# A two-layer hybrid diffusion step on one core: the order of instructions from another scheduling simulation

## The chip, the cores and the metric

The kernel runs on one core of a Trainium2 chip. The metric is the device time of one execution in microseconds; before the change it is 2791.19 us, the median of 3 runs (2787.31 to 2797.09). Five engines with a queue of instructions each work side by side: TensorE (PE; its weight loads are PEld), VectorE (DVE), ScalarE (ACT), GpSimd (POOL) and SyncE (SP), which here only issues DMAs. Each queue is executed in order, and engines wait for each other through semaphores.

## The reference, cut to what matters

128 context tokens and 128 latent tokens go through two trunk layers with one set of weights. All data is float32.

```python
def trunk_layer(x, cvec, p, l, rope, ctx):
    mods = (silu(cvec) @ p['ada_w'][l] + p['ada_b'][l])         # 6 vectors of 2048
    h = rmsnorm(x, p['norm1_g'][l]) * (1 + scale1) + shift1
    u = h @ p['w_in'][l]                                        # 2048 x 4960
    o_mla, ckv, kr = mla(u_mla, ...)                            # 8 heads, low-rank q and kv, softmax
    o_gdn, s_gdn = gated_deltanet(u_gdn, ...)                   # 4 heads, two directions, chunked delta rule
    o_ssd, s_ssd = mamba2_ssd(u_ssd, ...)                       # 8 heads, two directions, chunked scan
    mixed = concatenate([o_mla, o_gdn, o_ssd], -1) @ p['w_out'][l]
    x = x + gate1 * mixed
    h = rmsnorm(x, p['norm2_g'][l]) * (1 + scale2) + shift2
    gt, up = split(h @ p['ffn_w_gu'][l], 2, -1)                 # 2048 x 11264
    x = x + gate2 * ((silu(gt) * up) @ p['ffn_w_down'][l])      # 5632 x 2048
```

## The kernel before, in words

The activations lie transposed, features on the partitions and the 256 tokens along the free dimension, so a weight block is the stationary operand of a matmul and the tokens stream through.

*Weights.* A weight comes in units of at most 128x1024 floats. `unit` (L372) loads one from DRAM (`load`, L331, on SP's queue, tile `raw`, four buffers), and `split` (L357) makes two parts of it: ScalarE rounds it to the high part `w1` (L360), and VectorE or GpSimd subtracts that from the original to get the low part `w2` (L364); which of the two engines does it is fixed in the program by a share per stage. Each has three buffers. The activations have the same two parts, and a product takes three matmuls or, in the FFN's wide form, two (512 and 256 columns). All matmuls are issued by `mm` (L224, seen as L225). They accumulate in four PSUM banks `acc`; the small matmuls of the recurrences and of attention use three banks `mx`.

*Stages.* Layer 0's input projection lies between 0 and some 240 us, the rest of layer 0's mixing (state space scan, delta rule, attention, output projection) up to about 720 us, its FFN up to about 1490 us, layer 1's projection and mixing up to about 2060 us, and its FFN from there to the end. In the mixing stages chunks of weight matmuls stand beside the chains of the three head groups, some of which go through DRAM (the decay rows `gcd`, the blocks `sB`, `sZ`, `sW` of the triangular solve, the outputs `og`).

*Modulation vectors.* The product of the condition with `ada_w` is spread over the whole program. Some blocks go through TensorE (`ada_run`, L398, tiles `araw`, bank `ada`); the others are multiplied and summed on VectorE during the FFNs (`vec_sums`, L451, the instruction at L505, tile `junk`), paced by `tick` (L531) with constants per stage. Their loads are on SP's queue too, among those of the weights.

*What sets the order.* The program is written in Python in one order. The Tile framework then puts the instructions of each engine into the order in which they are queued. It goes forward in simulated time: when an engine is free in the simulation, it takes, of the instructions whose inputs are there in the simulation, the one of the best priority, and it hands out tile buffers as they come free. The priority is the place in the program; loads and splits of a unit, and the loads of `ada_w`, are put ahead of it (`tc.high_priority()`, L374, L392, L467). Some instructions are tied behind the one traced before them on their engine (`tc.keep_in_program_order`): the first loads (L336), the matmuls while `pinned["on"]` is set (L232: from the first norm until the end of layer 0's projection, and inside a run of `ada` matmuls), and the sums on VectorE (L504).

```python
    def unit(src, nk, n):
        with tc.high_priority():
            raw = raw_tile()
            load(out=raw[:, :nk * n], in_=src)
            w1, w2 = split(raw, nk * n)
```

The context that does this is opened at the end of `kernel` (L1575) without any option, so the simulation is the framework's default one (its core simulator).

## Time and profile before

| | us |
|---|---|
| median of 3 runs | 2791.19 |
| profiled execution | 2789.01 |
| its span, first to last instruction | 2787.2 |
| PE busy | 2624.7 (94%) |
| DVE busy | 1924.1 (69%) |
| ACT busy | 1261.9 (45%) |
| POOL busy | 753.6 (27%) |
| mean granted TensorE clock | 0.981 of full |

A busy share is a mean over all stages, and TensorE's matmuls are pipelined, so a stretch of 50 us with PE busy 100% can still hold fewer matmuls than another. The share of the whole span tells little here; the rows below go by stretch.

### The profile page before, as it was taken

To read this page: it belongs to the slowest core of one execution; us is meant where nothing else is said; L and a number is where in the kernel's file an instruction comes from. 1 tells how busy PE (TensorE), PEld (TensorE's weight loads), DVE (VectorE), ACT (ScalarE), POOL (GpSimd) and SP (SyncE) were. 2 spreads that over 40 slices of the span, in tenths; PEclk is the share of its full clock that TensorE was granted. 3 is DMA by queue.
4 is the path that set the end of the run, shared out by engine and by line. 5 is a ranking of instruction groups with operands and counts; after the bars stand their busy time and mean duration, and the time that the engine had idled before them with its cause. 6 is when DMAs were issued, how large, how long until landed. Compare 5 with 4: busy or idle time off the path is not lost. (4 is left out here: it accounts for less than half of the span.)

```text
span 2787.2 us, 45955 instructions
## 1 busy us (share of the span) xinstructions
PE 2624.7 (94%) x17856; PEld 2324.3 (83%) x17856; DVE 1924.1 (69%) x3162; ACT 1261.9 (45%) x1802; POOL 753.6 (27%) x415
## 2 busy tenths in 40 slices
PE   7988889999999999999999999999999999999999
PEld 5876767888887788788888888888988888888888
DVE  2657845454999899898986786555477777755444
ACT  4345605544444444444334563355454454444333
POOL 1121003222455555455554320231330000000000
PEclk9999999999999999999999999999999999999999
DMA  8988757456698888889985555343657777655554
GB/s 331 347 305 289 251 185 243 151 212 222 230 323 313 312 299 318 294 307 337 340 322 186 172 163 169 111 137 110 221 194 230 232 241 229 202 187 188 195 195 149
DMA packets 224107, 658.01 MB, mean 236 GB/s; under 512 B 34320, under 2 KB 61584, under 8 KB 223888
## 3 DMA queue, kind: packets, MB, share of 16 engines
q1 hardware_dynamic: 174384, 619.26, 64.1%
q10 hardware_dynamic: 49504, 35.81, 4.3%
q8 instruction: 140, 2.29, 0.3%
q14 instruction: 79, 0.65, 0.1%
HBM read 641.22 MB, written 13.76 MB: 235 GB/s over the span
## 5 line engine op out<-in xcount | busy, mean ns | idle before, releaser
L225 PE MATMUL acc<-h,w 128*128 128x256 f32 (+1 forms) x8960 | 1428.9, 320 | 54.2 <-DVE w L364 19.0
L225 PEld LDWEIGHTS acc<-h,w 128*128 128x128 f32 x8960 | 1273.2, 193 | 205.6 <-DVE w L364 29.0
L360 ACT ACTIVATE w<-raw 128x1024 fp32r<-128x1024 f32 (+2 forms) x811 | 828.6, 1025 | 889.1 <-PE acc L225 606.5
L364 DVE TENSOR_TENSOR w<-raw,w 128x1024 fp32r<-128x1024 f32 (+2 forms) x577 | 710.5, 1232 | 512.5 <-ACT w L360 503.6
L364 POOL TENSOR_TENSOR w<-raw,w 128x1024 fp32r<-128x1024 f32 (+3 forms) x234 | 569.2, 2434 | 993.1 <-ACT w L360 840.2
L505 DVE SCALAR_TENSOR_TENSOR junk<-araw,srep 128x1024 bf16<-128x1024 f32 x448 | 544.5, 1215 | 9.6 <-DMA araw<-ada_w 1.9
L225 PE MATMUL acc<-f,w 128*128 128x256 f32 (+1 forms) x2560 | 456.3, 340 | 3.6 <-DVE w L364 3.6
L225 PEld LDWEIGHTS acc<-f,w 128*128 128x128 f32 x2560 | 392.8, 189 | 64.3 <-DVE w L364 4.3
L225 PE MATMUL acc<-m,w 128*128 128x256 f32 x1536 | 191.8, 285 | 0.0
L225 PEld LDWEIGHTS acc<-m,w 128*128 128x128 f32 x1536 | 186.6, 192 | 2.9 <-issue 2.5
L1424 POOL TENSOR_TENSOR f<-sg,f 128x512 fp32r<-128x512 f32 x40 | 60.9, 1523 | 426.3 <-ACT f L1423 426.3
L225 PE MATMUL ada<-araw,sc 128*32 128x256 f32 x1280 | 88.3, 397 | 21.1 <-DVE mods L436 16.2
L225 PE MATMUL mx<-h,w 128*128 128x256 f32 (+1 forms) x672 | 90.7, 293 | 10.1 <-ACT w L360 5.2
L225 PEld LDWEIGHTS mx<-h,w 128*128 128x128 f32 (+1 forms) x672 | 85.7, 195 | 14.6 <-ACT w L360 6.2
L661 DVE SCALAR_TENSOR_TENSOR xT<-acc,mods,xT 128x128 f32<-128x128 f32 x192 | 53.9, 343 | 43.1 <-PE acc L225 35.5
L225 PEld LDWEIGHTS ada<-araw,sc 128*32 128x32 f32 x1280 | 37.6, 112 | 51.8 <-DVE mods L436 18.1
L1428 ACT ACTIVATE up<-acc 128x256 f32<-128x256 f32 x80 | 30.7, 384 | 107.6 <-PE acc L225 76.4
L648 ACT ACTIVATE h<-nt,mods 128x128 fp32r<-128x128 f32 x128 | 44.0, 392 | 63.7 <-DVE nt L647 62.5
L647 DVE SCALAR_TENSOR_TENSOR nt<-xT,modA,rstd 128x128 f32<-128x128 f32 x128 | 57.0, 482 | 7.4 <-ACT rstd L611 7.2
L1428 ACT ACTIVATE sg<-acc 128x256 f32<-128x256 f32 x80 | 29.9, 381 | 68.4 <-PE acc L225 68.4
L602 POOL TENSOR_TENSOR sqacc<-sqacc,sqt 128x256 f32<-128x256 f32 x39 | 39.9, 1022 | 74.0 <-ACT sqt L598 73.1
L1463 DVE TENSOR_TENSOR sg<-sg,up 128x256 f32<-128x256 f32 x80 | 57.8, 723 | 1.6
(296 smaller groups left out, 1971.6 us busy)
## 6 DMA issues: line engine op xcount, KB each, us to landing
araw<-ada_w SPq DMA_DIRECT2D x384, 512.0 KB, 5.4
raw<-ffn_w_gu SPq DMA_DIRECT2D x352, 512.0 KB, 4.4
raw<-ffn_w_down SPq DMA_DIRECT2D x165, 512.0 KB, 4.3
raw<-w_in SPq DMA_DIRECT2D x144, 512.0 KB, 4.6
raw<-w_out SPq DMA_DIRECT2D x64, 512.0 KB, 4.0
raw<-mla_w_uq SPq DMA_DIRECT2D x24, 384.0 KB, 3.1
raw<-mla_w_ukv SPq DMA_DIRECT2D x16, 512.0 KB, 3.7
araw<-srow SPq DMA_DIRECT2D x12, 512.0 KB, 5.7
```

What stands on the lines that cost most here:

```text
L225: return pin(PE.matmul(out, lhsT=lhsT, rhs=rhs, start=start, stop=stop, skip_group_check=True))
L360: S.activation(w1[:, :w], raw[:, :w], AF.Copy)
L364: e.tensor_tensor(w2[:, :w], raw[:, :w], f32(w1[:, :w]), op=ALU.subtract)
L505: V.scalar_tensor_tensor(junk, raw, 1.0, s[r], op0=ALU.mult, op1=ALU.mult, accum_out=sums[g][:, 2 * (c - g[1]) + t, r, h:h + 1]))
L602: G.tensor_tensor(sq["acc"], sq["acc"], t, op=ALU.add)
L647: V.scalar_tensor_tensor(t[:, c], X_["t"][:, kt, c], A[:, kt, g:g + 1], rstd[:, c], op0=ALU.mult, op1=ALU.mult)
L648: S.activation(h1[:, kt, c], t[:, c], AF.Identity, bias=B[:, kt, g:g + 1])
L661: V.scalar_tensor_tensor(xs, ps[:, i * T:(i + 1) * T], gates[:, kt, g:g + 1], xs, op0=ALU.mult, op1=ALU.add)
L1424: G.tensor_tensor(f[:, :, 1], sg_, f32(f[:, :, 0]), op=ALU.subtract)
L1428: S.activation(t, bank[:, NT:2 * NT], AF.Copy)
L1463: V.tensor_tensor(t[:, j], t[:, j], u, op=ALU.mult)
```

## The change

The context in which the kernel is traced is told to schedule with the framework's other simulation, the timeline simulation. Nothing else is changed: the traced program, its priorities, pins, pools and pace constants are the same.

```diff
-    with tile.TileContext(nc) as tc:
+    with tile.TileContext(nc, schedule_with_timeline_sim=True) as tc:
         build(tc, nc, aps)
```

## Rows read from the trace of the kernel before

**Rows 1.** Busy time by stretch; (x) are instructions, PEclk the granted clock.

```profile
core 0: us, PE busy (x) PEld busy (x) DVE busy (x) ACT busy (x) POOL busy (x), PEclk, DMA share, GB/s
0.00:50.00 50.00, 33.20 (x241) 23.63 (x242) 9.69 (x22) 19.43 (x36) 3.67 (x7) 0.90 0.82 317
50.00:350.00 300.00, 268.92 (x2497) 232.44 (x2495) 208.08 (x449) 149.17 (x221) 44.96 (x23) 0.96 0.83 303
350.00:400.00 50.00, 39.47 (x349) 32.26 (x350) 20.92 (x38) 1.36 (x4) 0.00 (x0) 0.90 0.74 228
400.00:750.00 350.00, 322.88 (x2549) 293.53 (x2548) 198.29 (x365) 161.77 (x287) 94.13 (x74) 0.97 0.59 199
750.00:1250.00 500.00, 473.72 (x2639) 403.81 (x2638) 462.57 (x692) 229.64 (x295) 275.04 (x121) 0.99 0.86 310
1250.00:1450.00 200.00, 198.70 (x1125) 172.07 (x1124) 177.60 (x296) 77.38 (x82) 112.45 (x54) 1.00 0.92 333
1450.00:1500.00 50.00, 46.20 (x252) 39.26 (x251) 28.09 (x58) 21.29 (x30) 26.17 (x14) 0.94 0.75 258
1500.00:2067.00 567.00, 525.82 (x4129) 505.11 (x4128) 376.89 (x680) 282.77 (x462) 154.12 (x101) 0.98 0.49 155
2067.00:2787.20 720.20, 715.77 (x4089) 622.17 (x4088) 441.92 (x568) 319.07 (x389) 43.05 (x24) 1.00 0.63 206
```

**Rows 2.** The chain that ended last, its longest pieces: start, us, what.

```profile
1953.39 72.04 PE acc L225 x598
2067.84 715.44 PE acc L225 x4086
```

**Rows 3.** Waits of PE from 50 to 350 us: us in total, times, longest.

```profile
PE ada L225 <- DVE mods L436: 15.6, 7, 4.7
```

**Rows 4.** Waits of PE from 750 to 1250 us.

```profile
PE acc L225 <- DVE w L364: 15.7, 13, 2.8
PE acc L225 <- POOL w L364: 10.4, 13, 1.6
```

**Rows 5.** Groups on DVE, 750 to 1250 us: busy us, mean ns | idle before.

```profile
L505 DVE SCALAR_TENSOR_TENSOR junk<-araw,srep 128x1024 bf16<-128x1024 f32 x252 | 306.4, 1216 | 6.8 <-DMA araw<-ada_w 1.9
L364 DVE TENSOR_TENSOR w<-raw,w 128x1024 fp32r<-128x1024 f32 x65 | 96.7, 1488 | 5.2 <-ACT w L360 4.9
L1463 DVE TENSOR_TENSOR sg<-sg,up 128x256 f32<-128x256 f32 x40 | 40.3, 1006 | 0.8
```

**Rows 6.** Single lines over the whole kernel: duration ns min/median/max.

```profile
L364 DVE TENSOR_TENSOR w<-raw,w x577: 539/1224/3346, 28.0 to 2779.6; 128x1024 fp32r<-128x1024 f32 x171, 128x512 fp32r<-128x512 f32 x13, 128x768 fp32r<-128x768 f32 x7, 128x384 fp32r<-128x384 f32 x2
L364 POOL TENSOR_TENSOR w<-raw,w x234: 1012/2405/3390, 42.2 to 2071.8; 128x1024 fp32r<-128x1024 f32 x111, 128x768 fp32r<-128x768 f32 x3, 128x384 fp32r<-128x384 f32 x2, 128x512 fp32r<-128x512 f32 x1
...
L1463 DVE TENSOR_TENSOR sg<-sg,up x80: 411/425/2674, 777.6 to 2537.2; 128x256 f32<-128x256 f32 x80
```

**Rows 7.** Order of time, 1034 to 1040 us: start, us, instruction [idle before].

```profile
1036.19 2.40 POOL L364 TENSOR_TENSOR w<-raw,w 128x1024 fp32r<-128x1024 f32 x1 [0.60 <-ACT w L360]
...
1036.35 3.33 DVE L364 TENSOR_TENSOR w<-raw,w 128x1024 fp32r<-128x1024 f32 x1
1039.60 1.21 DVE L505 SCALAR_TENSOR_TENSOR junk<-araw,srep 128x1024 bf16<-128x1024 f32 x1
1039.73 0.51 PE L225 MATMUL acc<-h,w 128*128 128x256 f32 x2 [0.80 <-DVE w L364]
```

**Rows 8.** Order of time of PE, 1500 to 2067 us: small groups between chunks.

```profile
1504.31 1.46 PE L225 MATMUL mx<-h,w 128*96 128x256 f32 x11
...
1569.03 0.65 PE L225 MATMUL mx<-da,cst 128*128 128x48 f32 x4 [0.62 <-DVE da L842]
...
1717.96 1.26 PE L225 MATMUL mx<-Z,Bp 128*128 128x128 f32 x8 [4.27 <-DMA Z<-sZ]
...
1949.25 0.41 PE L1346 MATMUL mx<-ident,r 128*128 128x128 f32 x2 [0.23 <-DVE r L1342]
...
2025.37 0.59 PE L225 MATMUL mx<-sqacc,ones 128*128 128x256 f32 x2
```

## Prediction

> **What bounds the kernel now.** I read four views in this order: busy time by stretch, who ended TensorE's waits, the groups of VectorE in the worst-fed stretch, and TensorE's order of time in one mixing stage.
>
> The stretches come first [rows 1]. TensorE is busy nearly all the time from 1250 to 1450 us and from 2067 us to the end, so nothing an order can do there gives much: the last 720.20 us hold 715.77 us of TensorE work. Its gaps lie elsewhere. They are the stretch length less PE busy: 16.8 us in the first 50, 31.1 in 50 to 350, 10.5 in 350 to 400, 27.1 in 400 to 750, 26.3 in 750 to 1250 and 41.2 in 1500 to 2067. With the 9.5 us in the three remaining stretches that is the 162.5 us in which TensorE does nothing. Beside the gaps stands the granted clock: 0.97 in 400 to 750 and 0.98 in 1500 to 2067. A mean of 0.97 says that six hundredths of the stretch ran at the lower of the two levels (1.2 instead of 2.4 GHz), and half of those are lost: 0.03 x 350 = 10.5 us, and 0.02 x 567 = 11.3 us.
>
> What TensorE does at full pace is in the chain of waits [rows 2]: 598 matmuls of w_out in 72.04 us, 120 ns each. The 4129 matmuls of 1500 to 2067 would need 497 us at that pace and take 567. The 70 us between are the 41.2 us of gaps and some 29 us in which TensorE is counted busy but runs slower, the 11.3 us of clock among them.
>
> So the kernel is bound by TensorE's own work, about 2.6 ms, and the order of instructions can only touch what hangs around it.
>
> **The change, part by part.** The flag adds and removes no arithmetic, no transfer and no matmul. The same simulated-time scheduler issues the same instructions; another simulation tells it when an input is ready and an engine free, and with that when a buffer is handed on. As the library describes the two, the new one prices the DMA engines, and the port that VectorE and GpSimd share, as things that are queued for; the old one prices each instruction by itself. What moves is the place of an instruction in its engine's queue, SP's and ScalarE's DMAs included. It matters only where the head of a queue waits while something behind it could run.
>
> *What can't move.* Until layer 0's input projection is done, matmuls are pinned to the order of the program; of the 31.1 us of gaps in 50 to 350, 15.6 us are seven pinned waits for the modulation vectors [rows 3]. I take 0 there; the bounds are 0 and 15.6 us. In the FFNs TensorE has nothing but the chunks of one chain, in the order of their accumulators, so its order stays; what can change is which VectorE, GpSimd and SP instruction runs first.
>
> *FFN of layer 0 (750 to 1250 us).* All its gaps are waits for a weight's low part: 15.7 us in 13 waits for VectorE's and 10.4 in 13 for GpSimd's [rows 4]. VectorE is at 462.6 of 500 us [rows 1]. Part of its time is stretched: the subtraction takes 1488 ns in the mean of 65 here, against a median of 1224 over the kernel, and the gate multiplication 1006 ns against 425 [rows 5, 6]. That is 65 x 0.264 + 40 x 0.581 = 40 us. One case shows how [rows 7]: GpSimd's subtraction starts at 1036.19 us, VectorE's at 1036.35 takes 3.33 us, and TensorE waits 0.80 us for it. An order that knows of this would move the subtractions of the two engines apart, or the low-priority sums behind them. The bounds: all of the 26.3 us gone, or 40 us more of stretched instructions, against 37.4 us of idle VectorE time, so next to nothing until that is used up and one for one beyond it. I take half the gaps, -13 us, because one half of them hangs on each of the two engines and an order serves one at a time.
>
> The Trainium skill speaks of this case, and against the change as much as for it (SBUF — State Buffer, "Who interferes with whom"): a VectorE instruction with two inputs in SBUF contends with a GpSimd instruction that reads SBUF, and whichever issues first blocks the other for its whole length. The 3.33 us row agrees [rows 7]. The mean does not go so far: GpSimd is busy in 275 of the 500 us, so by the rule 55% of the 65 subtractions would lose half of its 2.4 us in the mean, an estimate of 43 us where the rows show 17. By the rule the sum would have 26 us more at stake in this stretch, to either side, since by it the meetings of two queues set the price; the third rival is that case.
>
> *Mixing stage of layer 0 (350 to 750 us).* Gaps of 10.5 + 27.1 = 37.6 us [rows 1]. Here and in layer 1 small matmuls of the recurrences and of attention (banks "mx") are interleaved with the long weight chunks (banks "acc"), and the interleaving is what the simulation decides. I take a third, -12.5 us; bounds -37.6 and the loss below.
>
> *Mixing stage of layer 1 (1500 to 2067 us).* TensorE passes from chunk matmuls to a small group 73 times between the first and the last row shown; 16 of these begin with a wait (the first at 1569.03 us, the last at 1949.25), 25.2 us in sum, 1.58 us in the mean, the longest 4.27 us for a block that returns from DRAM [rows 8]. At such a place the old simulation believed the input to be there sooner than it was. Of the 41.2 us of gaps I take a third, -13.7 us. The rest are true latencies of the chain (a split or a convolution on VectorE that must be done in any order), or inputs of the chunks themselves. Bounds: -41.2 us, and +90 us if the 57 quiet places began to wait as the 16 do (57 x 1.58).
>
> *Clock.* The lower level stands in the same stretches as the gaps [rows 1]. If a third of the gaps goes, I let a third of its 21.8 us go with them: -7 us; bounds 0 and -21.8.
>
> *New waits.* No simulation meets the chip at the tenth of a microsecond, so some of the quiet places will wait. I charge ten of them at 1.58 us, +16 us, nearer to the 16 seen than to none or to 57.
>
> The sum: -13 - 12.5 - 13.7 - 7 + 16 = -30 us. The profiled execution took 2789.01 us (span 2787.2 and 1.8 us around it) and lies 2.2 us under the median of 2791.19. So 2759 us against the profiled time, and **2761 us** as a median of runs. If these stalls go, what is late next is the weights' low parts in the first FFN, and TensorE's own 2.6 ms.
>
> **The rivals.**
> *Stalls change places, or the order hardly changes.* 2791 us. For it: TensorE is pinned at the start and follows its chunks in both FFNs, some 1.7 of the 2.8 ms, and the pace constants stay. Against it: 73 places of choice in one stage alone, and VectorE's queue in the first FFN at 93%.
> *Small matmuls come to the head too early (slower).* Place: the mixing stages. Price: 1.58 us for each group that TensorE's queue reaches before its input. For it: the queue is in order, behind a waiting group stand ready chunk matmuls, and the paces in the program were set with the old order. Against it: the new simulation prices more of what made the 16 wait, the DMA round trip above all. It decides when more than 29 places begin to wait (29 x 1.58 = 46 us, the sum of the gains). If half of the 73 in layer 1 wait, 21 more, that is +33 us, and by the share of matmuls (2898 of 350 to 750 against 4129) +23 us in layer 0. With the 13 us of the FFN still gained that is +43: 2834 us.
> *VectorE and GpSimd meet more often in the first FFN (slower).* The stretched 40 us become 120. The first 37 us of it fill VectorE's idle time, the other 43 us are TensorE's: also 2834 us. For it: VectorE's queue is nearly full, so any wait is handed on. Against it: the new simulation prices just these meetings.
> *Most stalls go (faster by far).* Two thirds of 26.3 + 37.6 + 41.2 + 21.8 = 127 us, and no new waits: 85 us, 2706 us. For it: of the 16 waits none is for more than the arrival of one input. Against it: VectorE is at 93% in the FFN, and the chains of the recurrence stay.
>
> **How the numbers follow.** What a measurement of this kernel can tell from no change is about 0.3%, 8 us. My forecast has 0.45, with a range of its own of 2738 to 2780; the great gain 0.09, no change 0.13, the early small matmuls 0.24, the meetings on VectorE 0.09. So faster 0.54, same 0.13, slower 0.33. For 8 in 10 the range takes in the forecast, the great gain, no change and the larger part of the slower cases: 2705 to 2845 us.
>
> **What would show it.** Right: in 1500 to 2067 TensorE's gaps fall below 30 us and fewer than 16 of the small groups begin with a wait, above all the one for the block from DRAM; in the first FFN TensorE waits less than 20 us for low parts; the granted clock of both mixing stages rises. The second FFN keeps its 715 us. Wrong: gaps of the mixing stages above 80 us together, or waits for small groups' inputs in more than 45 places (slower by the second rival); the mean of VectorE's subtraction in the first FFN above 1.7 us (the third); or a new gap in the second FFN, which no part of the sum allows for.

## The result, and the profile after

The changed kernel takes 2725.68 us (median of 4 runs, 2723.08 to 2732.52), the kernel before 2794.14 us beside it (4 runs, 2787.31 to 2799.08). The ratio is 0.9768, 95% interval 0.9741 to 0.9795: faster by 2.3%. The medians lie 68 us apart; 30 us were forecast. The profiled execution of after took 2725.19 us with a span of 2723.4 us, 63.8 us less than the span before.

The first two fences give the busy time by stage, columns as in [rows 1], with the edges set at the same event in both kernels: the start of the first and the end of the last wide matmul of a gate and up part, and the last matmul of an FFN's down part. Only the first edge, 340 us, is a time and no event: the changed kernel has about 100 matmuls more before it, and so fewer in its first row. First the kernel before.

```profile
core 0: us, PE busy (x) PEld busy (x) DVE busy (x) ACT busy (x) POOL busy (x), PEclk, DMA share, GB/s
340.00:752.70 412.70, 371.26 (x2985) 331.10 (x2986) 230.90 (x443) 165.13 (x293) 95.79 (x75) 0.95 0.61 203
752.70:1237.00 484.30, 460.32 (x2562) 391.91 (x2562) 447.05 (x671) 222.46 (x286) 264.35 (x117) 0.99 0.87 311
1237.00:1490.70 253.70, 250.11 (x1411) 216.53 (x1410) 211.96 (x347) 99.47 (x107) 147.03 (x71) 0.99 0.89 318
1490.70:2082.10 591.40, 545.92 (x4268) 523.50 (x4266) 391.36 (x709) 295.34 (x483) 160.18 (x103) 0.97 0.50 159
2082.10:2534.40 452.30, 452.30 (x2563) 392.31 (x2562) 307.52 (x397) 216.60 (x281) 33.98 (x20) 1.00 0.67 219
```

The same stages after the change, in the same columns.

```profile
340.00:748.10 408.10, 366.28 (x2890) 333.53 (x2889) 254.89 (x494) 175.95 (x312) 99.05 (x77) 0.95 0.56 183
748.10:1196.20 448.10, 448.10 (x2565) 390.26 (x2564) 428.27 (x675) 222.50 (x286) 263.24 (x117) 1.00 0.93 339
1196.20:1442.50 246.30, 246.30 (x1410) 214.38 (x1408) 213.07 (x349) 100.30 (x107) 147.51 (x71) 1.00 0.91 327
1442.50:2023.00 580.50, 539.46 (x4266) 521.66 (x4266) 388.61 (x711) 295.48 (x481) 171.07 (x103) 0.97 0.51 162
2023.00:2470.70 447.70, 447.70 (x2563) 389.98 (x2562) 306.12 (x396) 215.72 (x281) 35.77 (x20) 1.00 0.67 221
```

The difference by stage: layer 0 up to its FFN -4.6 us (752.7 to 748.1), gate and up part of the first FFN -36.2, its down part -7.4, layer 1's mixing -10.9, gate and up part of the second FFN -4.6, the rest -0.1. Two thirds of the gain lie in the first FFN. There the length falls by 36.2 us, and TensorE's busy time by 12.2 us (460.32 to 448.10) with the same matmuls: 24 us are gaps that went, and in the other 12 us the same matmuls take less time. In the second FFN TensorE was busy all the time in both kernels, and still the same 2563 matmuls take 4.6 us less.

Waits that answer to [rows 4] do not exist any more: TensorE waits for nothing between 748.1 and 1442.5 us. ScalarE and SP show the change one step earlier. First before, gate and up part of the first FFN (SPq is SP's queue; "SPq L332 <- DVE junk" is a load that cannot be issued until a sum on VectorE has freed its tile).

```profile
SPq L332 <- DVE junk L505: 241.3, 102, 6.0
SPq L332 <- POOL w L364: 56.2, 36, 3.7
SPq L332 <- DVE w L364: 19.6, 15, 3.8
ACT w L360 <- PE acc L225: 58.9, 40, 3.5
ACT w L360 <- DMA raw<-ffn_w_gu: 54.8, 44, 4.3
```

The same part after.

```profile
SPq L332 <- DVE junk L505: 103.9, 72, 3.9
SPq L332 <- POOL w L364: 99.8, 73, 2.9
SPq L332 <- DVE w L364: 69.2, 49, 3.3
ACT w L360 <- PE acc L225: 86.6, 64, 1.8
ACT w L360 <- DMA raw<-ffn_w_gu: 22.0, 13, 3.4
```

SP waits 137 us less for the sums and 93 us more for the splits that free the weights' own tiles; ScalarE waits 33 us less for weights and 28 us more for TensorE to free `w1`. The weights are earlier now, and what ScalarE's rounding waits longest for is TensorE.

VectorE's groups that answer to [rows 5]: the mean of the subtraction falls from 1480 ns (64 between 752.7 and 1237 us) to 1333, that of the gate multiplication from 986 (38) to 824.

```profile
L505 DVE SCALAR_TENSOR_TENSOR junk<-araw,srep 128x1024 bf16<-128x1024 f32 x246 | 298.8, 1215 | 8.4 <-DMA araw<-ada_w 4.4
L364 DVE TENSOR_TENSOR w<-raw,w 128x1024 fp32r<-128x1024 f32 x64 | 85.3, 1333 | 4.2 <-ACT w L360 4.0
L1463 DVE TENSOR_TENSOR sg<-sg,up 128x256 f32<-128x256 f32 x38 | 31.3, 824 | 0.4
```

Of layer 1's small groups [rows 8], 9 of 70 now begin with a wait, 10.5 us in sum, against 16 of 73 and 25.2 us; the block from DRAM waits 2.31 us instead of 4.27. In layer 0's mixing (350 to about 745 us) it is 7 of 62 and 2.7 us against 13 of 49 and 19.5 us. Two of the nine:

```profile
1536.54 0.71 PE L225 MATMUL mx<-BC 128*128 128x128 f32 x4 [2.31 <-ACT BC L884]
...
1661.21 2.08 PE L225 MATMUL mx<-Z,Bp 128*128 128x128 f32 x8 [2.31 <-DMA Z<-sZ]
```

But both mixing stages pay for it. In layer 0 a run of four pinned `ada` blocks now waits for its loads: 15.3 us in 9 waits between 340 and 748 us, where before it was 3.0 us in 3.

```profile
PE ada L225 <- DMA araw<-ada_w: 15.3, 9, 6.0
```

There the chunk matmuls (bank `acc`) wait 19.8 us instead of 8.9. The gaps between 340 us and the FFN are 41.8 us in all, before 41.4: nothing of the small groups' gain is left in them. In layer 1 chunk matmuls wait 21.9 us instead of 16.4, and matmuls inside the small groups 8.5 us instead of 3.1, so that the stage's gaps fall by 4.5 us only, from 45.5 to 41.0.

The end of the chain of waits after, answering to [rows 2]: the w_out piece keeps its 120 ns a matmul, the last piece is 4.9 us shorter for one matmul less.

```profile
1908.82 57.13 PE acc L225 x476
2008.86 710.58 PE acc L225 x4085
```

### The profile page after: what moved, and what is told of

Read it like the earlier page. It is cut to its first block, busy times and chain, and to the rows that moved or that the text cites. A ratio compares the mean times of both kernels' runs of the same rounds, so it can differ in the third digit from the quotient of the medians.

```text
span 2723.4 us, 45875 instructions
## 1 busy us (share of the span) xinstructions
PE 2595.1 (95%) x17856; PEld 2314.6 (85%) x17856; DVE 1900.4 (70%) x3162; ACT 1249.6 (46%) x1793; POOL 769.3 (28%) x415
## 5 line engine op out<-in xcount | busy, mean ns | idle before, releaser
L225 PE MATMUL acc<-h,w 128*128 128x256 f32 (+1 forms) x8960 | 1410.4, 318 | 51.1 <-ACT h L648 17.6
L364 POOL TENSOR_TENSOR w<-raw,w 128x1024 fp32r<-128x1024 f32 (+3 forms) x234 | 576.8, 2467 | 979.5 <-ACT w L360 839.0
L225 PE MATMUL acc<-f,w 128*128 128x512 f32 (+1 forms) x2560 | 453.3, 339 | 0.0
L225 PE MATMUL acc<-c,w 128*128 128x256 f32 x288 | 56.2, 293 | 4.6 <-ACT c L1215 4.6
L651 DVE SCALAR_TENSOR_TENSOR h<-nt,mods,h 128x128 fp32r<-128x128 f32 x128 | 49.7, 431 | 8.8 <-ACT h L648 8.8
L422 ACT ACTIVATE adsb<-ada 128x256 f32<-128x256 f32 x24 | 9.1, 379 | 97.9 <-PE ada L225 77.8
```

Source lines behind the costliest of these rows:

```text
L225: return pin(PE.matmul(out, lhsT=lhsT, rhs=rhs, start=start, stop=stop, skip_group_check=True))
L364: e.tensor_tensor(w2[:, :w], raw[:, :w], f32(w1[:, :w]), op=ALU.subtract)
L422: S.activation(sb, ps, AF.Copy)
L651: V.scalar_tensor_tensor(h2[:, kt, c], t[:, c], B[:, kt, g:g + 1], f32(h1[:, kt, c]), op0=ALU.add, op1=ALU.subtract)
```

## The experiments

**One stage at a time, and the control.** All of these are the kernel of before with its default simulation. A table holds, for each engine, the changed kernel's order of traced instructions; order edges (no semaphores) tie each to the one ahead of it, inside one stage only. The other stages keep before's order in all but a few places.

```diff
+_ORDER = {"SP": "...", "DVE": "...", "PE": "...", "Activation": "...", "Pool": "..."}
+
+def _follow(tc, nc):
+    made = {}
+    for i in nc.cur_bb.bb.instructions:
+        made.setdefault(i.engine, []).append(i)
...
+        for i, j in zip(seq[1:], seq):
+            tc.add_manual_dep(i, j.name, edge, reason="order")
...
     with tile.TileContext(nc) as tc:
         build(tc, nc, aps)
+        _follow(tc, nc)
```

First FFN alone:

> The kernel of before (default simulation), with the five queues of the first FFN alone (about 750 to 1490 us) put into the order that the timeline simulation gave them; every other stage keeps the order of before. Theory A (each stage's order carries its own gain): the 44 to 48 us that lie between the two traces in this stage come, nothing else: 2794 - 46 = 2748 us, ratio 0.982 to 0.986, and the weight waits of TensorE in 750 to 1250 us are gone. Theory B (what a stage gains hangs on where the stages before it leave the weight queue and the tiles): less than half of it, over 2770 us.

Layer 0 up to its FFN alone:

> The same with layer 0's stages up to the start of its FFN alone. Theory A: between the traces this stage gave 4.6 us and took back none: 2786 to 2796 us, same as before, with the attention and state space work in the other's order and the nine new waits for the modulation vectors' loads (15 us) in 395 to 500 us. Theory B: the early part sets up the FFN, so some of the FFN's 46 us come here too, under 2780 us.

Layer 1's projection and mixing alone:

> The same with layer 1's projection and mixing alone (about 1490 to 2060 us). Theory A: 2794 - 11 = 2783 us, ratio 0.996. Theory B: nothing here without the new order ahead of it, 2790 us or more.

All stages:

> Control: default simulation, all five queues in all stages put into the order of the changed kernel by added order edges. If the order is all that the flag changes, the time is that of the changed kernel, 2718 to 2734 us, ratio 0.977 within 0.003. If something beside the order (where tiles lie, which waits are set) carries the gain, it stays well above, over 2745 us.

Measured, with the kernel before at 2789.09 us beside them:

| order of after in | median us | ratio, 95% interval |
|---|---|---|
| first FFN | 2742.24 | 0.983 [0.9802, 0.9857] |
| layer 0 before its FFN | 2780.37 | 0.9972 [0.9955, 0.9989] |
| layer 1's mixing | 2780.43 | 0.9964 [0.9947, 0.9981] |
| everywhere | 2724.92 | 0.9764 [0.9736, 0.9792] |

The stages' lengths in the profiled executions (us, edges as above):

| | up to the FFN | gate, up 0 | down 0 | mixing 1 | gate, up 1 | rest |
|---|---|---|---|---|---|---|
| before | 752.7 | 484.3 | 253.7 | 591.4 | 452.3 | 252.8 |
| after | 748.1 | 448.1 | 246.3 | 580.5 | 447.7 | 252.7 |
| first FFN | 746.1 | 450.7 | 245.8 | 591.2 | 452.4 | 252.7 |
| layer 0 before its FFN | 745.0 | 483.1 | 252.6 | 593.7 | 452.3 | 252.8 |
| layer 1's mixing | 758.6 | 482.5 | 251.3 | 579.3 | 452.3 | 252.8 |
| everywhere | 747.1 | 451.8 | 246.3 | 579.5 | 447.8 | 252.6 |

Theory A holds for the first FFN and for layer 1's mixing, and theory B falls: each stage's order brings a gain of its own, and no stage behind the first column moves by more than 2.4 us without its own new order. The three ratios multiply to 0.9767, where the changed kernel has 0.9768; so close a match is luck, since each ratio is known to 0.002 or 0.003 and the second FFN's 4.6 us are in none of the three. The control shows that the order alone is enough for the whole gain. Layer 0's run lies below the 2786 to 2796 us of theory A, at the border of theory B. By the repeated runs it gives about 8 us, and the trace has them in its own column and not in the FFN, as A says. A single trace can't size this column: with one and the same order it lies between 746.1 and 758.6 us from one profiled execution to the next.

The first FFN with the new order (TensorE waits 1.8 us in it):

```profile
746.10:1196.80 450.70, 448.96 (x2565) 390.05 (x2564) 434.22 (x675) 221.29 (x286) 266.69 (x117) 1.00 0.92 337
1196.80:1442.60 245.80, 245.80 (x1409) 214.22 (x1408) 213.08 (x349) 100.29 (x107) 147.44 (x71) 1.00 0.90 327
```

**Which queue in the first FFN.** That stage's order brought 47 us (2789.09 to 2742.24). The table is now cut to one engine; the other engines take the order that the simulation then finds for them.

```diff
-_ORDER = {"SP": "...", "DVE": "...", "PE": "...", "Activation": "...", "Pool": "..."}
+_ORDER = {"SP": "..."}
```

> Default simulation; in the first FFN only SP's queue (the loads) gets the order of the changed kernel, the other engines follow by themselves (VectorE's order stays three times nearer to before's than to the changed one's, 260 pairs turned round against 637). Theory S (the loads' order decides: weight loads stood behind loads of ada_w that wait for the sums on VectorE): most of the 47 us of this stage, 2742 to 2755 us, ratio 0.983 to 0.988, and ScalarE's waits for ffn_w_gu fall from 55 us to about 20. Theory V (VectorE's order decides: subtractions ahead of the sums): nothing, over 2775 us. Theory P (the two go together, each order is a half): 2760 to 2775 us.

With VectorE's order alone:

```diff
-_ORDER = {"SP": "..."}
+_ORDER = {"DVE": "..."}
```

> The same with VectorE's queue alone; SP's order ends between the two kernels (263 pairs turned round against before, 162 against the changed one). Theory S: by SP's pairs about half of the 47 us, 2760 to 2775 us. Theory V: all of it, 2740 to 2750 us. Theory P: 2750 to 2765 us.

And the reverse, the changed kernel with SP's old order in that stage:

```diff
     with tile.TileContext(nc, schedule_with_timeline_sim=True) as tc:
         build(tc, nc, aps)
+        _follow(tc, nc)
```

> The changed kernel (timeline simulation) with SP's queue of the first FFN put back into before's order; VectorE follows and ends nearer to the changed kernel's order (285 pairs against 578). Theory S: the 47 us are lost again, 2765 to 2775 us. Theory V: little is lost, 2726 to 2740 us. Theory P: 2740 to 2760 us.

With both, after the results of these three:

```diff
-_ORDER = {"SP": "..."}
+_ORDER = {"SP": "...", "DVE": "..."}
```

> Default simulation, in the first FFN the queues of SP and of VectorE together get the changed kernel's order. SP's alone gave nothing (2789.55 us) and VectorE's alone 8 us (2784.16 us). Theory P2 (two limits in a row: the loads must come before VectorE can be early, and VectorE must take the subtractions early for the loads to count): together nearly all of the 47 us, 2742 to 2752 us, ratio 0.983 to 0.987, TensorE's weight waits under 6 us. Rival: ScalarE's, GpSimd's or TensorE's order is needed as well: over 2765 us.

Measured, each ratio to the kernel before beside it (2791.91 us, and 2794.31 for the last run): SP's order alone 2789.55 us, ratio 0.999 [0.9978, 1.0003]; VectorE's alone 2784.16, 0.9972 [0.9956, 0.9988]; the changed kernel with SP's old order 2769.33, 0.9904 [0.987, 0.9938], 44 us above the changed kernel's 2725.68 by the medians and 38 us by the ratios; SP's and VectorE's together 2769.53, 0.992 [0.9895, 0.9945], 22 us. In the trace with SP's old order the first FFN takes 740.3 us (480.3 and 260.0), before 738.0 and after 694.4, so that this stage's gain is gone. No expected case held in all of these runs: SP's order alone came out as theory V has it, SP's old order as theory S, VectorE's order alone as none, and the two together as the rival, over 2765 us. Neither of these two queues carries the gain alone, yet taking SP's order back loses it. The traces of the gate and up part show where each stops (edges as above). With SP's order alone:

```profile
SPq L332 <- POOL w L364: 186.8, 90, 5.7
SPq L332 <- DVE junk L505: 28.3, 26, 2.9
ACT sg L1428 <- PE acc L225: 59.1, 20, 6.1
ACT up L1428 <- PE acc L225: 57.3, 21, 4.3
ACT w L360 <- DMA raw<-ffn_w_gu: 2.8, 2, 1.5
PE acc L225 <- POOL w L364: 10.9, 15, 1.7
PE acc L225 <- DVE w L364: 8.2, 8, 2.1
```

The loads are early (ScalarE waits 2.8 us for weights, before 54.8), but TensorE still waits 19 us for low parts: the weights lie in their tiles, and the roundings stand behind gate work that waits for TensorE's accumulators (116 us in "sg" and "up"). With VectorE's order alone the loads are late again:

```profile
ACT w L360 <- DMA raw<-ffn_w_gu: 63.7, 52, 3.2
PE acc L225 <- POOL w L364: 13.2, 16, 1.7
PE acc L225 <- DVE w L364: 3.8, 7, 1.3
```

With SP's old order in the changed kernel that wait is the largest of all runs:

```profile
ACT w L360 <- DMA raw<-ffn_w_gu: 132.4, 86, 4.9
```

With both queues TensorE's waits for low parts are 12.1 us, and ScalarE waits 91 us for TensorE in "sg" and "up", against 50 in the changed kernel:

```profile
752.00:1221.70 469.70, 456.45 (x2563) 390.91 (x2562) 432.34 (x669) 218.74 (x286) 265.83 (x117) 1.00 0.89 321
```

Its waits there:

```profile
ACT up L1428 <- PE acc L225: 57.4, 20, 4.3
ACT sg L1428 <- PE acc L225: 33.3, 16, 3.4
PE acc L225 <- POOL w L364: 8.7, 16, 0.9
PE acc L225 <- DVE w L364: 3.4, 7, 0.9
```

So a weight passes three queues in a row, SP's, ScalarE's and that of the subtracting engine, and each has other work that can stand ahead of it. Shown is that the gain is lost with SP's old order, though the other engines stay free to follow, and that SP's and VectorE's new orders are not enough. The two halves of TensorE's waits part here: those for VectorE's low parts fall from 13.4 us to 8.2, 3.8 and 3.4 in the three runs on the kernel of before, those for GpSimd's stay at 10.9, 13.2 and 8.7 (before 10.4), and only with all five queues do both go (1.6 and 0.2). What frees GpSimd's half is open. In the run with both orders GpSimd's own queue, left free, has only 6 pairs of instructions turned round against the changed kernel's (22 against before's), ScalarE's in 107 (171) and TensorE's in 909 (378), so ScalarE's and TensorE's orders are what is missing. That ScalarE's place of the rounding is the third limit is read from its waits; neither its order nor TensorE's was tried in this stage, alone or added to the two.

**TensorE's pace.** TensorE's order alone, in the second FFN:

```diff
-_ORDER = {"SP": "..."}
+_ORDER = {"PE": "..."}
```

> Default simulation; in the second FFN TensorE's matmuls alone get the changed kernel's order, in which about 80 neighbouring pairs of a 512-column and a 256-column matmul are swapped. Theory: matmuls of one width in a row run faster, so the gate and up part falls from 452.3 to about 448 us (4.6 us, 0.16% of the whole: 2789 to 2791 us, to be read from the trace). Rival: the pace comes from VectorE's or ScalarE's order, then it stays at 452 us.

2787.05 us, ratio 0.9989 [0.9975, 1.0004], not to be told from no change; but the trace has the gate and up part at 447.7 us, to the tenth the changed kernel's, with VectorE and ScalarE nearly in before's order:

```profile
2087.90:2535.60 447.70, 447.70 (x2563) 389.94 (x2562) 307.81 (x397) 216.67 (x281) 33.92 (x20) 1.00 0.66 221
```

The starts of single matmuls in the trace show how. A pair is one matmul of 512 columns (A) and one of 256 (b), each with other weights; the numbers are ns from its start to the next start.

```
before, repeated without end    A235 b114  A232 b118  A241 b120              3 pairs 1060, 353.3 each
TensorE's order of after        A236 b113  A233 b117  A241 b120              3 pairs 1060, 353.3
   after a swap of neighbours   A231 b112  A233 b117  A231 b113  A232 b118   4 pairs 1387, 346.8
512, 512, 256, 256 throughout   A233 A235 b117 b112  A233 A231 b113 b119     4 pairs 1393, 348.3
```

The swaps are not quick in themselves, as the expectation had it: each throws TensorE from one repeating cycle into another, and it stays there until the next swap. The changed kernel has such a place, two 512-column matmuls in a row, some 60 times in the second FFN, where the kernel before has none. This pointed to one edit more, made in both kernels:

```diff
                         if self.wide:
                             mm(v4(self.banks[j][:], 2), w1[:, i, o:o + m], self.r.both(k), first, False)
-                            mm(self.outs[j], w2[:, i, o:o + m], self.r.part(0, k), False, last)
                         else:
                             triple(self.outs[j], w1[:, i, o:o + m], w2[:, i, o:o + m], self.r, k, first and j % 2 == 0, last)
+                    if self.wide:
+                        for j, (o, m) in enumerate(self.tiles):
+                            mm(self.outs[j], w2[:, i, o:o + m], self.r.part(0, k), False, last)
```

> The changed kernel (timeline simulation) with one edit in the program: in the wide form of both FFNs the two 512-column matmuls of a weight row stand ahead of its two 256-column ones (512, 512, 256, 256 instead of 512, 256, 512, 256). In the traces TensorE repeats a cycle of 353 ns per pair in the order 512, 256, and after some swaps one of 346.5 ns. Theory: the pace hangs on the order, every unit runs at about 347 ns: 1280 pairs of the gate and up part from 447.7 to about 444 us, 704 of the last part from 353 to 347 ns, 4 us; in both FFNs together 14 us less, 2708 to 2716 us, ratio to before 0.970 to 0.973. Rival: a swap only knocks TensorE out of one cycle into another, and a regular 512, 512, 256, 256 settles in a cycle of its own at 353 or more: 2724 us or above.

> The same edit in the kernel of before (default simulation). Theory: the second FFN gains its full share, 452.3 to 444 us and 4 us in the last part, 12 us; in the first FFN TensorE waits for low parts, so the pace gives little, but the low parts are also wanted 120 ns later: 0 to 5 us. 2775 to 2782 us. Rival: as before, 2791 us.

On the changed kernel: 2716.77 us, ratio to before 0.9736 [0.9711, 0.9761], the fastest median of all. Its interval overlaps that of the changed kernel (0.9741 to 0.9795), so the traces must carry the comparison. Gate and up part and down part of both FFNs:

```profile
747.90:1194.70 446.80, 446.30 (x2561) 389.01 (x2561) 434.50 (x675) 221.71 (x285) 266.49 (x117) 1.00 0.93 339
1194.70:1440.70 246.00, 245.93 (x1413) 214.53 (x1411) 212.92 (x348) 100.71 (x107) 146.70 (x71) 1.00 0.90 328
2018.60:2464.60 446.00, 446.00 (x2562) 389.19 (x2562) 304.02 (x396) 213.87 (x280) 34.18 (x20) 1.00 0.66 222
2464.60:2714.50 249.90, 245.93 (x1411) 214.20 (x1409) 125.77 (x165) 95.22 (x101) 3.37 (x2) 1.00 0.56 184
```

Against after that is 1.3 + 0.3 + 1.7 + 2.8 = 6.1 us, less than half of the 14 expected: the regular order has a cycle of its own, 348 ns a pair, between the two. The span is 8.9 us shorter than after's; the other 2.8 us are outside the FFNs. On the kernel of before, 2780.8 us, ratio 0.9956 [0.9935, 0.9977]: its second FFN gains 9.4 us (452.3 to 445.8 and 252.8 to 249.9), and the first 5.5 (484.3 to 481.9 and 253.7 to 250.6), each within 3 us of what was expected.

The last run also shortens the pinned runs that wait for `ada_w`:

```diff
-            ada_pace(TM[0][0], TM[0][1], 4)
+            ada_pace(TM[0][0], TM[0][1], 2)
...
-            ada_pace(TM[1][0], TM[1][1], 4)
+            ada_pace(TM[1][0], TM[1][1], 2)
```

> e3_pairs with the modulation vectors of layer 0's and layer 1's mixing taken in runs of 2 weight blocks instead of 4, so that a pinned run can wait for two loads at most. Theory: the 15.3 us that TensorE waits for these loads between 395 and 500 us (9 waits) fall to half, 6 to 8 us under e3_pairs. Rival: the loads come late because SP's queue is held up by other waits (15.8 us for one), and shorter runs wait as often: no change against e3_pairs.

2721.06 us, ratio 0.9742 [0.9714, 0.977]: no change against 2716.77. The waits only fall from 14.4 us (9) to 10.5 (8). That fits the rival, loads that SP issues late: between 340 and 520 us SP waits 41.2 us for subtractions to free tiles, 15.1 in one piece, and without this edit 40.0 and 15.0.

## Why the prediction was right, and where its sum was not

The direction and the kind of mechanism were right: the order alone moves the time, through the waits at the heads of queues. The size came out at more than twice the forecast, inside the range but below the forecast's own 2738 to 2780 us. The first FFN was mis-sized; the other terms nearly add up (-17.2 us with the clock and the new waits, -15.5 measured in the two mixing stages), and that is luck, as the steps show.

*FFN of layer 0, "I take half the gaps, -13 us":* This term was mis-sized: it measured -36.2 in the gate and up part and -7.4 in the down part. Two things were missing. All gaps went, not half (23.8 us of waits before 1237 us and 3.6 behind it, to nothing): that an order serves one of the two subtracting engines at a time is what the runs with one or two queues show, but the whole new order served both. And TensorE's busy time fell by 12.2 us, for which the sum had no term. Of these, 3.4 us are the granted clock. It was at the lower level for 6.8 us before, and nowhere in this part after.

```profile
1145.40:1152.30 6.90, 6.13 (x20) 5.28 (x21) 5.18 (x9) 2.64 (x3) 3.62 (x2) 0.51 0.56 194
```

The other 8.8 us can be split by an estimate. The second FFN does the same matmuls in nearly the same old order with no wait in 452.3 us; down to there are 4.6 us, which went with the waits, and from there to 448.1 another 4.2, near the 4.6 that TensorE's own order gave in the second FFN. In the first FFN that order was not tried alone.

*"In the FFNs ... its order stays", "the second FFN keeps its 715 us."* Wrong. Two 512-column matmuls stand in a row some 250 times in the first FFN after the change (36 before) and some 60 times in the second (none before), and the second FFN's piece of the chain fell from 715.44 to 710.58 us.

*Mixing of layer 1, -13.7 us:* -10.9 by the trace and 10 us by its own run (0.9964). The waits at the heads of small groups fell as the text said they would, in fewer than 16 places, by 14.7 us; the block from DRAM gave 2.0 us of it, not the most. But other waits took back 10 us, so the stage's gaps only fell from 45.5 to 41.0 us (for the 4129 matmuls of the sign's own stretch from 41.2 to 35.9), not below 30. The other 6.5 us are busy time of TensorE; why it fell is open.

*Mixing of layer 0, -12.5, and new waits, +16:* the two belong together. Waits at the heads of small groups fell by 16.8 us, 6.1 of it at the block from DRAM. Waits of `ada` matmuls for `mods` gave another 5.9. The pinned `ada` runs took back 12.3 (3.0 to 15.3) and the chunk matmuls 11, so the gaps from 340 us on did not fall at all (41.4 to 41.8). The new waits are no quiet small groups that began to wait, as the term had it: they stand in a place that the text had only looked at as already pinned, and in the chunks of both layers. Counted from the start, gaps fell by 2.2 us (85.5 to 83.3) and busy time by 2.4, which makes the 4.6 us of the trace; the repeated runs say about 8.

*Clock, -7 us:* nothing. The granted clock of both mixing stages stayed, 0.95 and 0.97, though waits of small groups went. Where the new `ada` waits lie, between 400 and 450 us, it even fell from 1.00 to 0.80. What the clock gave lay in the first FFN, where the sum had not looked for it.

*The rivals.* "Stalls change places" is what happened in layer 0, and to two thirds of what the small groups gave in layer 1. The early small matmuls did not come: 70 switches with 9 waits. VectorE and GpSimd met about as often, but lost less by it: 31 of the 102 subtractions and gate multiplications of the gate and up part began while GpSimd ran, after the change 30, and what they took beyond 1224 and 425 ns fell from 37.7 to 22.2 us. The Trainium skill's rule on the shared port (SBUF — State Buffer, "Who interferes with whom": whichever issues first blocks the other for its whole length) would give, as an estimate with GpSimd busy 263 of 448 us and half of its 2.4 us lost at each meeting, a subtraction of 1.9 us in the mean; the trace has 1.33. Nor does the rule hold for every instruction with two inputs in SBUF: the sums have two as well, 142 of the 244 before began while GpSimd ran, and none took more than 1224 ns. Here the measurement decides.

```profile
L505 DVE SCALAR_TENSOR_TENSOR junk<-araw,srep x244: 1203/1220/1224, 753.5 to 1236.9; 128x1024 bf16<-128x1024 f32 x122
```

And the meetings were not the price of this stage. With SP's and VectorE's order the stretched time is 27.1 us (first two lines), no more than the 28.4 us with the first FFN's whole order (last two lines), and yet the gate and up part takes 469.7 us against 450.7.

```profile
L364 DVE TENSOR_TENSOR w<-raw,w 128x1024 fp32r<-128x1024 f32 x64 | 87.9, 1373 | 23.5 <-ACT w L360 23.4
L1463 DVE TENSOR_TENSOR sg<-sg,up 128x256 f32<-128x256 f32 x38 | 33.7, 886 | 0.4
L364 DVE TENSOR_TENSOR w<-raw,w 128x1024 fp32r<-128x1024 f32 x64 | 86.7, 1355 | 1.9 <-ACT w L360 1.7
L1463 DVE TENSOR_TENSOR sg<-sg,up 128x256 f32<-128x256 f32 x38 | 36.2, 952 | 0.4
```

Which of the new simulation's prices leads to the better order, that of the DMA engines or that of the shared port, no run here shows.

*The signs.* Two of the signs of being right came: 9 small groups of layer 1 that begin with a wait instead of 16, and no wait of TensorE for low parts in the first FFN. Three did not: layer 1's gaps below 30 us, a higher clock in the mixing stages, 715 us for the second FFN. None of the signs of being wrong came (the gaps of both mixing stages are 74 us in the stretches that answer to the prediction's, under its 80).

What could have been seen beforehand: ScalarE's 54.8 us of waits for `ffn_w_gu` and SP's 241.3 us for `junk` were in the trace of before, two steps ahead of the waits of [rows 4]. Followed back, they say that loads of the sums stand in front of the weights' loads, so that the order of other queues than VectorE's and GpSimd's was at stake. That all 26 us would go they do not say: with SP's order alone ScalarE's waits for weights were gone, and the time did not move.

## What to carry to other kernels

When TensorE waits for a prepared operand, follow that operand back through every queue it passes and note what else stands in each; an order that mends one queue alone may show nothing (SP's: 0.999), because the next one holds the weight up. A scheduler's other simulation can be tried in one line, and its order can be imposed stage by stage afterwards to see which stages earn it. Gaps of TensorE at 0% do not mean that its pace is the best: look at start to start times of single matmuls as well.

## What the runs showed of the hardware

A stream of 512 and 256 column matmuls with a weight load each falls into one of several repeating cycles, 346.8, 348.3 or 353.3 ns for a pair, at full granted clock and with no wait. Which one depends on the order of the matmuls and on what came before. In the second FFN's gate and up part 1.4% hang on it: 353.4 ns a pair before (452.3 us for 1280), 348.4 with 512, 512, 256, 256 (446.0 us). Why the cycles differ was not found.

VectorE's subtraction of two tiles of 128x1024 floats is lengthened when it begins while GpSimd runs: 15 of 64 did so in the first FFN's gate and up part before, at 2.33 us in the mean, and the other 49 took 1.22 us. VectorE's sums, which multiply two tiles of the same size and add up the products, are not: 1.20 to 1.22 us, 142 of 244 with GpSimd running at their start.
